# Weight sums of the projection pairs tied behind the C22 add, two mixed sums made in place, and one product's weight split on VectorE

## The chip, the cores and the metric

The kernel runs on one core of one Trainium2 chip. A core has five engines that this text speaks of: PE (TensorE, the matmuls), DVE (VectorE), ACT (ScalarE), POOL (GpSimd) and SP, which here only issues DMA transfers. Each engine works through its own instructions in order and waits on semaphores for the others. The metric is the device time of one execution in microseconds (us).

## The reference

Four layers over 1024 tokens of width 1024, all in fp32: an attention layer, a pooling layer, a mixer of two branches (neighbourhood attention and a gated recurrence, with 16 meta tokens put ahead of the sequence), and an MLP. The change concerns the pooling layer and three large projections of the rest:

```python
def pool_layer(h, w_in, w_mix, scale, w_out):
    u, z = jnp.split(h @ w_in, [POOL_WIDTH], axis=-1)
    p = multiscale_pool(u)          # per group: window sums of 2, 4, 8, 16 tokens / count - u
    m = jnp.einsum('bsgc,gcd->bsgd', p, w_mix).reshape(B, S, POOL_WIDTH) * scale
    return (m * jax.nn.silu(z)) @ w_out
...
    h = h + mix @ w_o[l]
    m = rms_norm(h, norm_mlp[l])
    h = h + jnp.square(jax.nn.relu(m @ w_up[l])) @ w_down[l]
```

## The kernel before

An fp32 operand X is held as two parts: hi, an ACT cast to a reduced fp32 form ("whi" for weights, "xh" for activations), and lo = X - hi ("wlo", "xl"), made by DVE or POOL. `mm3` makes a product from three matmuls, hi·hi, hi·lo and lo·hi. In the profile L108 is hi·hi, L110 and L111 are the two mixed ones. `split_evac` makes both parts; `split_b` (L249) does so for two halves of a weight block, its low part on POOL unless another engine is named.

Large products are done by seven block products in place of eight (Winograd's form of Strassen): with A cut into four blocks, S1 = A21 + A22, S2 = S1 - A11, S3 = A21 - A11, S4 = A12 - S2, the same kind of sums for the weights, and sums of the products for the result's blocks C11, C12, C21, C22.

**Input projections** (`project_pairs`, used for the pool layer's w_in with 8 pairs and for w_up with 16). A pair is 2 × 128 output columns. Its two products with A11 and A12 (`first_two`) come early for the first pairs (NF = 5 in the pool layer, 4 in the up projection), otherwise just ahead of the pair. Then, per pair, PE does S2, S1, S3, S4 and A22, twelve matmuls each. `weight_sums` (L361) makes the pair's four weight sums on DVE, from the raw weights that SP has loaded; `split_group` (L272) makes their parts, whi on ACT (L275), wlo on POOL (L276). Behind S3 DVE adds the bank to C22 (`res.add(p, "22", ...)`, L226 in the pool layer, L1853 in the up projection). The A22 product goes into the same bank, so PE waits for that add. The order in which DVE gets sums and adds is set by the code's order, a scheduler's priorities, and `tc.issue_after(x)`, which ties what is issued in it behind instruction x. For the first NF pairs x was the sums of the previous pair:

```python
                with tc.issue_after(ready.pop(p)):
                    done = weight_sums(r1, r2, tt)
                if p + 1 < NF:
                    ready[p + 1] = done
```

**The pool layer.** Even pairs give u, odd pairs silu(z); ACT copies banks (L898), the class `Pooled` cuts the window sums into small steps on DVE that it puts between the pair's instructions (`steps`), ending in a split ("cut", L950). After two pairs `mix` (L957) multiplies with w_mix, scales on DVE (L966), and makes the blocks of the next product's operand for a quarter q: A11, A12, A22 and S1 to S4, which it stores to memory (d_m). For the last quarter all of these went to memory too, and the output projection loaded S2, S1 and A22 whole into three tiles "ub" (`load_m`, 1 MB each).

**The output projections** (pool layer from L1080, w_o from L1797): seven products of 24 matmuls for the first and 24 for the second weight half, as three loops `times`; `split_a` makes the activations' parts, `less` the weight differences on DVE, `add_p` adds the banks to x. The third product takes S2 and w11 - w12. `made[0]` is the last low part that `split_a` made. In the pool layer the meta tokens' norm (an ACT square at L1107, and Newton steps of a reciprocal root on DVE, L124 to L132) stands between.

Of the kernel before, what the change touches and what calls it, by code (L numbers as in the profile page):

```python
# [19 lines left out]
P = 128  # L20
# [10 lines left out]
def fused_kernel(tc, a, out, stop=None, dbg=None):  # L31
# [295 lines left out]
    def project_pairs(w, col, npr, xx, sh, gcol, rows, a11, a12, stage, raw_tile, opened, res, w0, scaled, NF):  # L327
# [89 lines left out]
        for j in range(4):  # L417
            if j < 3:
                banks[j + 1] = [turned(rows[4:], j + 1 + k) for k in (0, 4)]
            if 0 < j < NF:  # L420
                open_[j] = first_two(j, wf[j])
            rest = sums(j)
            if j < 3:
                rest()
            if j == 0:
                split_first(2)
                split_first(3)
                if NF > 4:
# [399 lines left out]
    with ExitStack() as ph:  # L828
# [34 lines left out]
        class Pooled:  # L863
# [29 lines left out]

            def copy(self, p, key, ps):
                if key != "11":
                    self.steps(1)
                c_ = ea[:, p - 2, :] if p in EARLY and key == "11" else self.dst(p, key)
                nc.scalar.copy(out=c_, in_=ps)  # L898
                return c_
# [57 lines left out]
        def mix(g, q):  # L957
# [4 lines left out]
            for j, h in ((0, 0), (1, 0), (0, 1), (1, 1)):  # L962
# [13 lines left out]
            for n, c_, x_, y_, op in (("S3", m[0, 0], m[0, 1], m[0, 0], ALU.subtract),  # L976
                                      ("S1", m[0, 1], m[0, 1], m[1, 1], ALU.add), ("S2", s2, m[1, 1], m[0, 0], ALU.add),
                                      ("S4", m[1, 0], m[1, 0], s2, ALU.subtract)):
                vec(c_, x_, y_, op)
                nc.sync.dma_start(out=d_m[n][:, q, :], in_=c_)  # L980

# [30 lines left out]
        def load_x(h, ch):  # L1012
            for t in range(4 * h, 4 * h + 4):
                nc.sync.dma_start(out=X.at(t, ch), in_=d_x1[t][:, ch * 512:ch * 512 + 512])

        load_x(0, 0)
# [5 lines left out]
        ring = {}  # L1022

        def load_m(n):
            ring[n] = mp.tile([P, 4, 512], F32, name="ub", bufs=3)
            nc.sync.dma_start(out=ring[n], in_=d_m[n])

        load_m("S2")
        load_m("S1")
        load_x(0, 1)  # L1030
        load_m("A22")
        load_x(1, 1)
# [11 lines left out]
        def add_p(banks, h, ch, done=False, rows=range(4)):  # L1044

            for i in rows:
                t = 4 * h + i
                dst = X.at(t, ch)
                vec(dst, dst, banks[i], ALU.add)
                if done:  # L1050
# [50 lines left out]
        C = banks4()  # L1101
        times(C, *ops, True)
        ops = split_a("xl0", in_two(ring["S4"])), split_b(w22)
        with tc.issue_after(made[0].ins):
            mj = ea[:, 1:, :].rearrange("p a b -> p (a b)")
            sm_ = small.tile([P, 1], F32, name="ss")
            nc.scalar.activation(out=mj[:NM], in_=mt[:NM], func=AF.Square, accum_out=sm_[:NM])  # L1107
# [6 lines left out]
        for i in range(2):  # L1114
            split_evac(*t4[i], w21[i])
        add_p(C, 0, 1, True)
# [608 lines left out]
    with ExitStack() as ph:  # L1725
# [356 lines left out]
```

## Time and profile before

| what | value |
|---|---|
| median of the runs | 2394.87 us (2392.39 to 2399.99, 3 runs) |
| profiled execution | 2395.45 us |
| its span | 2393.6 us, 32247 instructions |
| mean granted TensorE clock | 0.984 |
| PE busy | 2290.5 us (96%) |
| DVE, ACT, POOL busy | 1509.4, 1021.5, 802.7 us |
| pool layer's input projection, from about | 470 to 680 us |
| its output projection | 680 to 780 us |
| w_o projection | 1640 to 1720 us |
| up projection, from about | 1765 us |

In the timelines a row is: start, duration, engine, line, operation, out<-in (partitions × elements, type), count, and in brackets the engine's idle time ahead of it and what ended it. A busy PE matmul of 512 columns lasts 0.39 us in the profile, but they overlap: one starts every 0.227 us when nothing is late.

### The profile page before, as it was taken

To read this page: it belongs to the slowest core of one execution; us is meant where nothing else is said; L and a number is where in the kernel's file an instruction comes from. 1 tells how busy PE (TensorE), PEld (TensorE's weight loads), DVE (VectorE), ACT (ScalarE), POOL (GpSimd) and SP (SyncE) were. 2 spreads that over 40 slices of the span, in tenths; PEclk is the share of its full clock that TensorE was granted. 3 is DMA by queue.
4 is the path that set the end of the run, shared out by engine and by line. 5 is a ranking of instruction groups with operands and counts; after the bars stand their busy time and mean duration, and the time that the engine had idled before them with its cause. 6 is when DMAs were issued, how large, how long until landed. Compare 5 with 4: busy or idle time off the path is not lost. (4 is left out here: it accounts for less than half of the span.)

```text
span 2393.6 us, 32247 instructions
## 1 busy us (share of the span) xinstructions
PE 2290.5 (96%) x11910; PEld 1904.0 (80%) x11910; DVE 1509.4 (63%) x2732; ACT 1021.5 (43%) x1921; POOL 802.7 (34%) x527
## 2 busy tenths in 40 slices
PE   7999999989988999999999999999889999999997
PEld 6877878767767888888988888887767888878886
DVE  5566676797678355554165746758784444686775
ACT  5344452643345354553232322423565555533334
POOL 2112133333433244331222112125414444454445
PEclk9999999989989999999999999999999999999999
DMA  5111113423372322211111111467135444764331
GB/s 159 36 28 36 28 32 106 145 67 119 101 252 79 93 58 54 67 50 54 45 45 53 49 53 49 135 197 266 64 121 198 149 147 167 257 227 167 106 123 71
DMA packets 249230, 254.41 MB, mean 106 GB/s; under 512 B 61096, under 2 KB 183038, under 8 KB 244848
## 3 DMA queue, kind: packets, MB, share of 16 engines
q1 hardware_dynamic: 240256, 234.69, 30.1%
q10 hardware_dynamic: 8224, 16.00, 1.7%
q0 software_dynamic: 592, 1.65, 0.4%
q8 instruction: 94, 1.54, 0.3%
q14 instruction: 64, 0.52, 0.1%
HBM read 182.05 MB, written 70.25 MB: 105 GB/s over the span
## 5 line engine op out<-in xcount | busy, mean ns | idle before, releaser
L108 PE MATMUL mm<-xh,whi 128*128 128x512 f32 (+2 forms) x1616 | 624.4, 387 | 18.2 <-DVE u L226 5.4
L110 PE MATMUL mm<-xl,whi 128*128 128x512 f32 (+2 forms) x1616 | 617.6, 382 | 0.0
L111 PE MATMUL mm<-xh,wlo 128*128 128x512 f32 (+2 forms) x1616 | 614.5, 380 | 1.9 <-POOL wlo L80 1.9
L80 POOL TENSOR_TENSOR wlo<-wraw,whi 128x1024 fp32r<-128x1024 f32 (+1 forms) x99 | 235.8, 2385 | 739.9 <-ACT whi L79 676.0
L108 PEld LDWEIGHTS mm<-xh,whi 128*128 128x128 f32 x1616 | 307.3, 190 | 77.0 <-DVE u L226 6.3
L111 PEld LDWEIGHTS mm<-xh,wlo 128*128 128x128 f32 x1616 | 306.9, 190 | 60.8 <-POOL wlo L80 2.7
L110 PEld LDWEIGHTS mm<-xl,whi 128*128 128x128 f32 x1616 | 307.4, 190 | 51.2
L111 PE MATMUL mm<-whi,xl 128*128 128x512 f32 (+1 forms) x752 | 273.3, 363 | 0.0
L79 ACT CAST whi<-wraw 128x1024 fp32r<-128x1024 f32 (+1 forms) x99 | 101.1, 1023 | 264.0 <-PE mm L110 146.0
L110 PE MATMUL mm<-wlo,xh 128*128 128x512 f32 (+1 forms) x560 | 196.9, 352 | 2.8 <-POOL wlo L80 1.4
L108 PE MATMUL mm<-whi,xh 128*128 128x512 f32 (+1 forms) x560 | 196.8, 352 | 2.5 <-DVE x L526 1.0
L108 PE MATMUL mm<-whi,xl 128*128 128x512 f32 x416 | 165.0, 398 | 13.5 <-ACT whi L118 8.2
L110 PE MATMUL mm<-wlo,xl 128*128 128x512 f32 x416 | 164.5, 396 | 10.7 <-POOL wlo L119 10.7
L276 POOL TENSOR_TENSOR wlo<-raw,whi 128x1024 fp32r<-128x1024 f32 (+1 forms) x59 | 121.5, 2059 | 137.8 <-ACT whi L275 137.7
L111 PEld LDWEIGHTS mm<-whi,xl 128*128 128x128 f32 x752 | 143.0, 190 | 22.1
L119 POOL TENSOR_TENSOR wlo<-wraw,whi 128x1024 fp32r<-128x1024 f32 x34 | 95.3, 2807 | 103.4 <-ACT whi L118 98.0
L110 PEld LDWEIGHTS mm<-wlo,xh 128*128 128x128 f32 x560 | 105.9, 189 | 17.8 <-POOL wlo L80 2.0
L108 PEld LDWEIGHTS mm<-whi,xh 128*128 128x128 f32 x560 | 105.9, 189 | 17.2 <-DVE x L526 1.4
L276 POOL TENSOR_TENSOR wlo<-wraw,whi 128x1024 fp32r<-128x1024 f32 (+1 forms) x28 | 70.9, 2534 | 136.5 <-ACT whi L275 109.0
L108 PEld LDWEIGHTS mm<-whi,xl 128*128 128x128 f32 x416 | 79.6, 192 | 32.3 <-ACT whi L118 7.7
L110 PEld LDWEIGHTS mm<-wlo,xl 128*128 128x128 f32 x416 | 79.6, 191 | 29.4 <-POOL wlo L119 13.1
L226 DVE TENSOR_TENSOR st<-st 128x512 f32<-128x512 f32 x64 | 63.2, 1008 | 56.7 <-ACT st L1928 55.6
(434 smaller groups left out, 4590.0 us busy)
## 6 DMA issues: line engine op xcount, KB each, us to landing
wraw<-in_w_in_dram SPq DMA_DIRECT2D x48, 512.0 KB, 3.7
d_S<-st SPq DMA_DIRECT2D x64, 256.0 KB, 4.5
raw<-in_w_up_dram SPq DMA_DIRECT2D x30, 512.0 KB, 5.4
d_A<-st ACTq DMA_DIRECT2D x48, 256.0 KB, 2.0
fa<-d_S SPq DMA_DIRECT2D x10, 1024.0 KB, 4.7
fa<-d_A SPq DMA_DIRECT2D x9, 1024.0 KB, 6.0
wraw<-in_attn_w_in_dram SPq DMA_DIRECT2D x32, 256.0 KB, 2.9
xh<-in_w_down_dram SPq DMA_DIRECT2D x16, 512.0 KB, 5.5
```

The source lines that it names most:

```text
L79: nc.scalar.copy(out=hv[:, i:i + n], in_=view[:, i:i + n])
L80: nc.gpsimd.tensor_tensor(out=lv[:, i:i + n], in0=view[:, i:i + n], in1=f(hv[:, i:i + n]), op=ALU.subtract)
L108: nc.tensor.matmul(ps, lhsT=lh[0], rhs=rh[0], start=first and i == 0, stop=False, skip_group_check=chain)
L110: nc.tensor.matmul(ps, lhsT=lh[0], rhs=rh[1], start=False, stop=False, skip_group_check=chain)
L111: nc.tensor.matmul(ps, lhsT=lh[1], rhs=rh[0], start=False, stop=last and i == n - 1, skip_group_check=chain)
L119: return (lo_eng or nc.vector).tensor_tensor(out=lo, in0=src, in1=f(hi), op=ALU.subtract)
L226: return nc.vector.tensor_tensor(out=out_, in0=x_, in1=y_, op=op)
L276: nc.gpsimd.tensor_tensor(out=lv, in0=view, in1=f(hv), op=ALU.subtract)
```

## The change

1. The weight sums of every pair (from the second on) are tied behind the C22 add of the pair before, in both input projections.
2. Pool layer: a bank is copied ahead of the pooled steps, not behind the first of them.
3. Pool layer, last quarter: S2 and S1 are written by DVE into the "ub" tiles themselves, and A22's quarter is copied there from its tile; the first three quarters are loaded ahead of the last mix.
4. The third product's low weights are made by DVE in place of POOL, in both output projections.
5. In the pool's output projection some DVE and ACT work is put or tied behind the banks' adds (`added`) or the last split (`made`): the splits of S3 and A22, the meta tokens' norm, two weight differences, the split of t4.

```diff
@@ project_pairs
-                ready = {1: weight_sums(*r0)}
+                weight_sums(*r0)
+                ready = {}
...
                 with tc.issue_after(ready.pop(p)):
-                    done = weight_sums(r1, r2, tt)
-                if p + 1 < NF:
-                    ready[p + 1] = done
+                    weight_sums(r1, r2, tt)
...
             res.add(p, "22", c22, b_)
-            if p + 1 >= NF:
-                ready[p + 1] = added[0].ins
+            ready[p + 1] = added[0].ins
@@ Pooled.copy
+                c_ = ea[:, p - 2, :] if p in EARLY and key == "11" else self.dst(p, key)
+                nc.scalar.copy(out=c_, in_=ps)
                 if key != "11":
                     self.steps(1)
-                c_ = ea[:, p - 2, :] if p in EARLY and key == "11" else self.dst(p, key)
-                nc.scalar.copy(out=c_, in_=ps)
@@ mix
-                            nc.sync.dma_start(out=d_m[n][:, q, :], in_=m[j, h])
-            s2 = s_tile()[:, :512]
+                            nc.sync.dma_start(out=d_m[n][:, q, :] if q < 3 else ring[n][:, 3, :], in_=m[j, h])
+            s2, s1 = [ring[n][:, 3, :] for n in ("S2", "S1")] if q == 3 else (s_tile()[:, :512], m[0, 1])
...
+                if q < 3 or n in ("S3", "S4"):
+                    nc.sync.dma_start(out=d_m[n][:, q, :], in_=c_)
@@ pool layer, output projection
+        for n in ("S2", "S1", "A22"):
+            load_m(n, 3)
         mix(GO[3], 3)
...
-        ops = o6, split_b(w11)
+        ops = o6, split_b(w11, nc.vector)
         o5 = split_a("xh0", in_two(ring["S1"]))
         load_m("S3")
-        less(w21, w21, w11)
-        less(w11, w22, w11)
+        with tc.issue_after(made[0].ins):
+            less(w21, w21, w11)
+            less(w11, w22, w11)
...
-        o4 = split_a("xh1", in_two(ring["A22"]))
...
-        with tc.issue_after(made[0].ins):
+        add_p(C, 1, 1)
+        times(C, *ops, False, True)
+        with tc.issue_after(added[0].ins):
+            o7 = split_a("xl1", in_two(ring["S3"]))
+            o4 = split_a("xh1", in_two(ring["A22"]))
             mj = ea[:, 1:, :].rearrange("p a b -> p (a b)")
...
-        add_p(C, 1, 1)
-        times(C, *ops, False, True)
-        ops = split_a("xl1", in_two(ring["S3"])), split_b(w12)
+        ops = o7, split_b(w12)
...
-            split_evac(*t4[i], w21[i])
+        with tc.issue_after(made[0].ins):
+            for i in range(2):
+                split_evac(*t4[i], w21[i])
@@ w_o, output projection
-        ops = o6, split_b(w11)
+        ops = o6, split_b(w11, nc.vector)
```

The lines of the changed kernel are one to two lower than before's between L434 and about L1100, and one higher behind.

DVE at pair 0 of the pool's input projection, before: the sums of pair 1 (raw_5247, wraw_5333, raw_5245) and of pair 2 (raw_5286, wraw_5451, raw_5318), and pair 0's C22 add, u_5266 with bank mm_4949.

```order
L226 TENSOR_TENSOR raw_5247<-raw_5247 128x512
L119 TENSOR_TENSOR s4l_4939<-sum_5014,s4h_4938 128x512
L226 TENSOR_TENSOR wraw_5333<-raw_5245,raw_5247 128x512
L226 TENSOR_TENSOR wraw_5333<-raw_5247,wraw_5333 128x512
L226 TENSOR_TENSOR raw_5245<-raw_5245,wraw_5333 128x512
L226 TENSOR_TENSOR raw_5286<-raw_5286 128x512
L226 TENSOR_TENSOR wraw_5451<-raw_5318,raw_5286 128x512
L226 TENSOR_TENSOR wraw_5451<-raw_5286,wraw_5451 128x512
L226 TENSOR_TENSOR u_5266<-u_5266,mm_4949 128x512
L226 TENSOR_TENSOR raw_5318<-raw_5318,wraw_5451 128x512
```

The same place now:

```order
L119 TENSOR_TENSOR s4l_4939<-sum_5014,s4h_4938 128x512
L226 TENSOR_TENSOR u_5266<-u_5266,mm_4949 128x512
L226 TENSOR_TENSOR raw_5247<-raw_5247 128x512
L226 TENSOR_TENSOR wraw_5333<-raw_5245,raw_5247 128x512
L226 TENSOR_TENSOR wraw_5333<-raw_5247,wraw_5333 128x512
L226 TENSOR_TENSOR raw_5245<-raw_5245,wraw_5333 128x512
L226 TENSOR_TENSOR u_5266<-u_5266,mm_5249 128x512
```

The add has moved ahead of all sums, and the sums of pair 2 have left this place.

DVE ahead of the third product of the pool's output projection, before: xl1 is the low part of S2 (loaded into ub_6433), wraw_6333 and wraw_6334 the two halves of w11, xh0_6588 the low part of S1, raw_63xx with mm the adds of the first product's banks.

```order
L226 TENSOR_TENSOR raw_6372<-raw_6372,mm_6456 128x512
L226 TENSOR_TENSOR raw_6369<-raw_6369,mm_6457 128x512
L119 TENSOR_TENSOR xl1_6519<-ub_6433,xl1_6519 128x1024 x2
L241 TENSOR_TENSOR wraw_6333<-wraw_6333,w12_6332 128x1024
L241 TENSOR_TENSOR wraw_6334<-wraw_6334,w12_6332 128x1024
L119 TENSOR_TENSOR xh0_6588<-ub_6435,xh0_6588 128x1024 x2
L241 TENSOR_TENSOR w21_6330<-w21_6330,wraw_6333 128x1024
```

Now (ub_6377 is S2, ub_6379 S1; z_6236 and z_6195 are tiles of the last mix):

```order
L226 TENSOR_TENSOR z_6195<-z_6195 128x512
L226 TENSOR_TENSOR ub_6379<-z_6195,z_6236 128x512
L226 TENSOR_TENSOR ub_6377<-z_6236,z_6195 128x512
L241 TENSOR_TENSOR w12_6332<-w12_6332,w22_6331 128x1024
L226 TENSOR_TENSOR z_6236<-z_6236,ub_6377 128x512
L241 TENSOR_TENSOR w12_6332<-w12_6332,w22_6331 128x1024
L119 TENSOR_TENSOR xl1_6516<-ub_6377,xl1_6516 128x1024 x2
L226 TENSOR_TENSOR raw_6369<-raw_6369,mm_6450 128x512
L226 TENSOR_TENSOR raw_6370<-raw_6370,mm_6451 128x512
L226 TENSOR_TENSOR raw_6371<-raw_6371,mm_6452 128x512
L226 TENSOR_TENSOR raw_6372<-raw_6372,mm_6453 128x512
```

S2's split has moved ahead of the first product's adds, right behind the sums that write it; the weight differences, half a split of S1 and the two low weight parts (wlo_6578, wlo_6582) follow there.

ACT at the same place, before:

```order
L118 CAST xh0_6337<-z_6195 128x512
L118 CAST whi_6509<-w21_6330 128x1024
L118 CAST xl0_6338<-z_6240 128x512
L118 CAST whi_6513<-w21_6330 128x1024
L1107 ACTIVATE ea_4192,ss_6745<-sum_6432 16x1024
L118 CAST xl1_6519<-ub_6433 128x1024 x2
```

and now:

```order
L118 CAST xh0_6337<-z_6195 128x512
L118 CAST whi_6506<-w21_6330 128x1024
L1109 ACTIVATE ea_4192,ss_6799<-sum_6435 16x1024
L118 CAST xl0_6338<-z_6236 128x512
L118 CAST whi_6510<-w21_6330 128x1024
L118 CAST xl1_6516<-ub_6377 128x1024 x2
```

The square of the meta tokens (L1107, now L1109) has moved ahead of the cast of xl from the last mixed tile.

More of the change, by code (lines that the diff above doesn't have):

```diff
@@ L973, in mix @@
                         if v == (j, h):
-                            nc.sync.dma_start(out=d_m[n][:, q, :], in_=m[j, h])
-            s2 = s_tile()[:, :512]
+                            nc.sync.dma_start(out=d_m[n][:, q, :] if q < 3 else ring[n][:, 3, :], in_=m[j, h])
+            s2, s1 = [ring[n][:, 3, :] for n in ("S2", "S1")] if q == 3 else (s_tile()[:, :512], m[0, 1])
             for n, c_, x_, y_, op in (("S3", m[0, 0], m[0, 1], m[0, 0], ALU.subtract),
-                                      ("S1", m[0, 1], m[0, 1], m[1, 1], ALU.add), ("S2", s2, m[1, 1], m[0, 0], ALU.add),
+                                      ("S2", s2, m[1, 1], m[0, 0], ALU.add), ("S1", s1, m[0, 1], m[1, 1], ALU.add),
                                       ("S4", m[1, 0], m[1, 0], s2, ALU.subtract)):
                 vec(c_, x_, y_, op)
-                nc.sync.dma_start(out=d_m[n][:, q, :], in_=c_)
+                if q < 3 or n in ("S3", "S4"):
+                    nc.sync.dma_start(out=d_m[n][:, q, :], in_=c_)
         wv = w_pout.rearrange("(q j p) c -> p q j c", j=2, p=P)
@@ L1014, in load_x, with load_m @@
                 nc.sync.dma_start(out=X.at(t, ch), in_=d_x1[t][:, ch * 512:ch * 512 + 512])
+        ring = {}
+        def load_m(n, nq=4):
+            ring[n] = mp.tile([P, 4, 512], F32, name="ub", bufs=3)
+            nc.sync.dma_start(out=ring[n][:, :nq, :], in_=d_m[n][:, :nq, :])
         load_x(0, 0)
+        for n in ("S2", "S1", "A22"):
+            load_m(n, 3)
         mix(GO[3], 3)
@@ L1021, in fused_kernel @@
         fg, mt = [s_tile()[:, :D] for _ in range(2)]
[L1022 to L1029, printed above, removed]
         load_x(0, 1)
-        load_m("A22")
         load_x(1, 1)
@@ L1048, in add_p @@
                 dst = X.at(t, ch)
-                vec(dst, dst, banks[i], ALU.add)
+                added[:] = [vec(dst, dst, banks[i], ALU.add)]
                 if done:
@@ L1109, in fused_kernel @@
             nc.vector.tensor_scalar_mul(mt[:NM], mt[:NM], r[:NM])
-        add_p(C, 1, 1)
-        times(C, *ops, False, True)
-        ops = split_a("xl1", in_two(ring["S3"])), split_b(w12)
+        ops = o7, split_b(w12)
         t4 = list(zip(*[in_two(mp.tile([P, 4, 512], F32R, name=n, bufs=b)) for n, b in (("ub", 3), ("w22", 1))]))
-        for i in range(2):
-            split_evac(*t4[i], w21[i])
+        with tc.issue_after(made[0].ins):
+            for i in range(2):
+                split_evac(*t4[i], w21[i])
         add_p(C, 0, 1, True)
```

## The prediction

> **What bounds the kernel now.** I read the page first, then the table of stretches, then the list of who waits for whom, and last the timeline of single engines around each wait. The first row of the page names the engine, and the table of stretches (microseconds of the stretch, then busy time of each engine, granted TensorE clock, DMA share, GB/s) shows where it is not full.
>
> ```profile
> PE 2290.5 (96%) x11910; PEld 1904.0 (80%) x11910; DVE 1509.4 (63%) x2732; ACT 1021.5 (43%) x1921; POOL 802.7 (34%) x527
> ```
>
> ```profile
> 470.00:680.00 210.00, 189.64 (x776) 151.60 (x775) 161.05 (x185) 83.43 (x122) 82.58 (x41) 0.94 0.37 114
> 680.00:780.00 100.00, 85.45 (x374) 68.60 (x373) 82.63 (x106) 50.84 (x95) 32.67 (x13) 0.93 0.43 147
> 780.00:1640.00 860.00, 847.56 (x5030) 728.62 (x5029) 474.73 (x986) 320.13 (x697) 230.08 (x189) 1.00 0.25 78
> 1640.00:1720.00 80.00, 68.13 (x280) 54.39 (x279) 63.72 (x59) 30.63 (x41) 52.08 (x20) 0.94 0.39 146
> 1765.00:1900.00 135.00, 127.53 (x544) 103.26 (x543) 74.65 (x95) 73.67 (x111) 56.98 (x27) 0.97 0.47 158
> ```
>
> PE is busy 96% of the span, and the long stretch from 780 to 1640 loses 12 us of 860 at clock 1.00. The four other stretches lose 20, 15, 12 and 7 us of idle time in 525, at a lower clock. They are the pool layer's input projection (470 to 680), its output projection (680 to 780), the w_o projection (1640 to 1720) and the up projection (from 1765), where the change acts. What PE waited for (total, times, longest):
>
> ```profile
> PE mm L110 <- POOL wlo L119: 11.7, 6, 6.9
> ...
> PE mm L108 <- ACT z L898: 5.8, 2, 3.9
> ...
> PE mm L108 <- DVE st L1853: 3.6, 3, 2.6
> ```
>
> A stall costs more than its length. Start times in the PE timeline, before, in and behind the stall at 511:
>
> ```profile
> 508.81 0.39 PE L111 MATMUL mm<-s4h,wlo 128*128 128x512 f32 x1
> ...
> 510.85 0.39 PE L111 MATMUL mm<-s4h,wlo 128*128 128x512 f32 x1
> 516.19 0.79 PE L108 MATMUL mm<-xh,whi 128*128 128x512 f32 x1 [4.95 <-DVE u L226]
> ...
> 522.22 0.39 PE L111 MATMUL mm<-s2h,wlo 128*128 128x512 f32 x1
> ```
>
> The nine steps from 508.81 to 510.85 are 0.227 us each. The fourteen from 516.19 to 522.22 take 6.03 us instead of 3.18: 2.85 us lost behind a gap of 5.34.
>
> **The weight sums of the pairs.** The four sums of pair p+1 used to follow those of pair p; now they wait for the C22 add of pair p. In pair 0 DVE did this:
>
> ```profile
> 509.92 2.86 DVE L226 TENSOR_TENSOR wraw<-raw 128x512 f32<-128x512 f32 x1
> 512.82 2.71 DVE L226 TENSOR_TENSOR wraw<-raw,wraw 128x512 f32<-128x512 f32 x1
> 515.46 0.67 DVE L226 TENSOR_TENSOR u<-u,mm 128x512 f32<-128x512 f32 x1
> ```
>
> Two sums of later pairs, stretched to four times their usual 0.68, stood ahead of the add that PE needed. With the add first, 5.1 us of the gap and the 2.85 us of slow matmuls go: 8 us. But the sums now start later, and pair 1's S2 product needs them through the add, the sums, the ACT cast and POOL's low part. Pair 7, whose sums were tied this way already, prices that chain:
>
> ```profile
> 638.03 0.69 DVE L226 TENSOR_TENSOR u<-u,mm 128x512 f32<-128x512 f32 x1 [2.75 <-PE mm L111]
> ```
>
> ```profile
> 642.01 3.50 POOL L276 TENSOR_TENSOR wlo<-wraw,whi 128x1024 fp32r<-128x1024 f32 x1 [3.43 <-ACT whi L275]
> ```
>
> From 638.03 to 645.5 are 7.5 us. Pair 7 hides them under its two opening products; the early pairs (pool 1 to 4, up 1 to 3) have their openings behind them, so the cover is S4, A22 and two matmuls of S2, 26 of 0.227 or 5.9 us. Odd pairs get a stall of 1.6 us; even pool pairs have a mix in between, 24 matmuls, that covers it. The mixes pay otherwise. POOL's low part now falls beside the pooled chain's two-input DVE work, which last time cost this, a 1.2 us split stretched to 3.1 and a PE wait behind it:
>
> ```profile
> 534.76 3.10 DVE L119 TENSOR_TENSOR u<-u,sum 128x1024 fp32r<-128x1024 f32 x1 [0.22 <-ACT sum L118]
> ```
>
> ```profile
> 537.91 0.49 PE L110 MATMUL mm<-u,whi 128*128 128x512 f32 x1 [1.87 <-DVE u L119]
> ...
> 539.18 0.63 PE L110 MATMUL mm<-u,whi 128*128 128x512 f32 x1
> ```
>
> On POOL the clearing of the next u tile, which waits for that split, now stands ahead of the mix weights' low part. I charge each of the first two mixes 2 us, one such wait (0 to 4), the odd pairs 1 and 3 together 3.2, and 1.6 us, a little over half of 2.85, for a slow pace behind one of these: 8.8 against 8 saved in pair 0. Pool pairs: 1 us lost (6 won if no new stall shows, 5 lost if both mixes pay 4).
>
> In the up projection PE waits for the same kind of add (st, L1853: 3.6 us in three waits). The longest, with the weight sum that stood ahead of its add:
>
> ```profile
> 1807.17 0.69 DVE L226 TENSOR_TENSOR wraw<-raw 128x512 f32<-128x512 f32 x1 [1.18 <-DMA raw<-in_w_up_dram]
> ```
>
> ```profile
> 1809.84 0.50 PE L108 MATMUL mm<-xh,whi 128*128 128x512 f32 x1 [2.60 <-DVE st L1853]
> ```
>
> The adds move ahead of the sums, so this wait of 2.6 us and the rest, 1.0 at most, go. But the long one mostly changes its place: its sums wait for a load that lands at 1807.1, and from there the chain (7.5 us less the add's 0.7) ends at 1813.9 at the worst, 2.4 sooner at the best with POOL and ACT free; without the stall S2's third matmul, 14 of 0.227 behind an A22 that starts at 1807.2, would be due at 1810.3. Gain 0.5 us (2 lost to 2 won).
>
> **S2 and S1 in place, and the third product's split.** The third product of the pool's output projection waited behind this chain (ACT, DVE, POOL, PE):
>
> ```profile
> 677.56 0.62 ACT L118 CAST xl<-z 128x512 fp32r<-128x512 f32 x1 [2.31 <-DVE z L966]
> ...
> 690.43 1.06 ACT L1107 ACTIVATE ea<-sum 16x1024 f32<-16x1024 f32 x1 [9.28 <-DMA sum<-in_meta_tokens_dram]
> ...
> 697.11 1.99 ACT L118 CAST xl<-ub 128x1024 fp32r<-128x1024 f32 x2 [5.53 <-DMA ub<-d_mS]
> ```
>
> ```profile
> 686.49 2.47 DVE L226 TENSOR_TENSOR raw<-raw,mm 128x512 f32<-128x512 f32 x4
> ...
> 698.19 2.36 DVE L119 TENSOR_TENSOR xl<-ub,xl 128x1024 fp32r<-128x1024 f32 x2 [5.21 <-ACT xl L118]
> ```
>
> ```profile
> 684.19 0.53 POOL L1037 DMA_DIRECT2D sum<-in_meta_tokens_dram  x1
> ```
>
> ```profile
> 673.48 0.39 PE L111 MATMUL mm<-sum,wlo 128*128 128x512 f32 x1
> ...
> 695.94 0.39 PE L111 MATMUL mm<-whi,xl 128*128 128x512 f32 x1
> ...
> 706.24 0.80 PE L110 MATMUL mm<-wlo,xl 128*128 128x512 f32 x1 [0.82 <-POOL wlo L119]
> ```
>
> The round trip of S2 through memory, ended at 697.1, goes: DVE writes the last quarter into the ring. What is late next is ACT: the meta tokens' square (L1107, now L1109) stands ahead of the cast of xl from z, and waits for a transfer that lands 6.2 us after POOL issues it (684.19 to 690.4). POOL issues it when the last mix's tiles are read, at 673.7, so it lands at 679.9; square 1.1, cast 0.6: DVE's low part of xl, due right behind the cast of 677.56, starts at 681.6. Five 128x512 instructions of 0.7 (that split and the four quarter sums) and two weight differences of 1.2 follow, with one stretch of 2.2 beside POOL's low part (as at 509.92); then the S2 split 2.36, four adds 2.47, two weight differences (128x1024 in two halves, so 2.36 again), a half split 1.2 and the first low weights 1.2: 699.3. That is 7 us ahead of 706.24. PE still stalls 3.4 us from 695.94, and its slow clock stays.
>
> The fifth product waited for C's adds, which stood behind two splits and the meta norm's Newton steps on DVE:
>
> ```profile
> 733.26 0.67 DVE L226 TENSOR_TENSOR z<-z,mm 128x512 f32<-128x512 f32 x1
> ```
>
> ```profile
> 728.67 0.39 PE L111 MATMUL mm<-whi,xh 128*128 128x512 f32 x1
> 734.07 0.76 PE L108 MATMUL mm<-whi,xl 128*128 128x512 f32 x1 [5.02 <-DVE w L128]
> ...
> 737.17 0.39 PE L110 MATMUL mm<-wlo,xl 128*128 128x512 f32 x1
> ```
>
> Now the adds come first: 5.2 us of the gap go, and 1.5 more, since the seven steps from 734.07 to 737.17 took 3.1 us instead of 1.6. Together 13.7 on PE, but the work passed over has to be done before the layer's norms, and DVE is busy 82.6 of the stretch's 100 us. I let 11 through (7 if only the third product's part reaches the norms, 14 if DVE hides all).
>
> In the w_o projection only the split's engine changes:
>
> ```profile
> 1674.62 9.59 POOL L119 TENSOR_TENSOR wlo<-wraw,whi 128x1024 fp32r<-128x1024 f32 x2 [5.47 <-issue]
> ```
>
> ```profile
> 1675.06 2.34 DVE L119 TENSOR_TENSOR xh<-a,xh 128x1024 fp32r<-128x1024 f32 x2
> ```
>
> ```profile
> 1674.55 0.48 PE L108 MATMUL mm<-whi,xl 128*128 128x512 f32 x1
> 1681.93 0.79 PE L110 MATMUL mm<-wlo,xl 128*128 128x512 f32 x1 [6.90 <-POOL wlo L119]
> ```
>
> DVE now makes half of the split at 1675.06, then the first low weights: 1675.06 + 1.2 + 1.2 = 1677.4 against 1681.9, so 4.5 us (3 if DVE is stretched by another 1.5, 6 if 1.5 of slow matmuls goes too). The second half comes two such steps later, and 24 matmuls of the first half, 5.4 us, cover it. PE's gap becomes 2.9 us; the wait of 1.9 at 537.91 was followed by matmuls of 0.63 at 539.18, so I keep the slow clock. The Trainium skill, "TensorE: Matmul & The Clock Gate", Part 1, lets the clock drop only after an idle window of about 3.4 us, which this row contradicts. By that rule the gap of 2.9 us here and the 3.4 left ahead of the third product would cost nothing behind them.
>
> Pool's bank copies put ahead of the pooled steps gain nothing: on ACT the copies still stand behind the split's cast at pairs 5 and 7, so the 5.8 us on L898 stay.
>
> Sum against the profiled execution of 2395.45 (span 2393.6 and 1.85 around it; 0.6 above the median 2394.87): 11 + 4.5 + 0.5 - 1 = 15. That gives 2380.4, or 2379.9 on the median's scale; I say 2380.
>
> **Rivals.** *All pair stalls go*: the new chains stay under cover, pool pairs win 6, up 2, the projection 13: 25 us, 2370. For it speaks that pair 7's 7.5 us contains a stretched POOL instruction; against it, pooled work that now lies exactly there. *Short gaps at full clock*: gaps up to 3.4 us are followed by matmuls of 0.39 at once, against the row at 539.18; two such gaps give 1.5 each, the charge of 1.6 in pool pairs falls away too: 4.6 us more, 2375. This is what the rule of the Trainium skill named above ("TensorE: Matmul & The Clock Gate", Part 1) comes to here. *ACT holds up the third product*: the square's transfer lands 4 us later than worked out, the third product starts at 703.3, and DVE's backlog of those 4 us makes the fifth and the norms as late again, 5 in all: 15 - 9 = 6, or 2389. It is decided at 681.6: each microsecond later there is one later on PE. *Slower*: the tied sums' chain, in the five pairs without cover (pool 1 and 3, up 1 to 3) and the two mixes. Once it exceeds 7.8 us, PE's wait exceeds 1.9 and the slow pace follows. With POOL's low part at 4.8, as in the two of 1674.62, instead of 3.5, the chain is 8.8: 2.9 and 2 of slow matmuls in each of five, 24.5, and the mixes 4 each, 32.5; less 8 and 2.6 of stalls removed, 22 lost against 15.5 won in the projections: 6.5 slower, 2401. Against it: only the pool's DVE is that crowded, and 638.03 shows 7.5 there. *The change doesn't do what it says*: the copies above are such a part, with no price.
>
> **Chances.** Forecast 0.58 (8 to 23 us won: 2372 to 2387), all stalls go 0.12, full clock 0.06, third product held up 0.12, slower 0.07, none of these 0.05. The range 2366 to 2392 takes in the first four. A measurement can tell 0.3%, about 7 us, from no change. Faster: 0.58 + 0.12 + 0.06 and a part of the held-up case, 0.78; same 0.15; slower 0.07.
>
> **What would show it.** Right: no PE gap at pair 0's A22 product, short waits on POOL's L276 at S2 of odd pairs; the third product starting near 699 with its low weights from DVE; no gap ahead of the fifth; a gap of 3 us instead of 7.4 in w_o. Wrong: PE gaps above 2.3 us at three or more S2 products; the mixes waiting above 4 us; the cast of xl from z after 684.

## The result and the profile after

The changed kernel takes 2381.62 us (2379.26 to 2383.87), the kernel before 2394.93 in the same job: a ratio of 0.9942, 95% interval 0.9923 to 0.9961, 13.3 us. A second job gave 2383.16 against 2392.71, 0.9959 (0.9945 to 0.9972). The profiled execution has a span of 2380.7 us against 2393.6. The first row of its page, then three of the stretches of the prediction (busy time of PE, PEld, DVE, ACT, POOL, granted clock, DMA share, GB/s):

```profile
PE 2284.9 (96%) x11910; PEld 1898.1 (80%) x11910; DVE 1505.3 (63%) x2736; ACT 1022.0 (43%) x1921; POOL 782.3 (33%) x523
```

```profile
470.00:680.00 210.00, 186.99 (x780) 148.32 (x779) 159.64 (x187) 85.05 (x125) 81.72 (x43) 0.97 0.38 120
680.00:780.00 100.00, 90.66 (x414) 73.59 (x414) 84.78 (x142) 54.73 (x104) 23.50 (x10) 0.97 0.37 133
1640.00:1720.00 80.00, 72.96 (x319) 58.52 (x318) 66.84 (x70) 37.89 (x57) 37.21 (x16) 0.98 0.32 118
```

PE starts 40 more matmuls than before in the 100 us from 680, 39 more in the 80 from 1640, but only 4 more in the 210 from 470: the gain is in the two output projections. What PE waits for now:

```profile
PE mm L108 <- ACT z L894: 8.3, 3, 3.9
...
PE mm L111 <- POOL wlo L276: 5.9, 7, 1.3
PE mm L1074 <- DVE sum L1111: 5.5, 1, 5.5
PE mm L110 <- POOL wlo L119: 5.4, 4, 2.0
...
PE mm L108 <- ACT whi L79: 4.0, 2, 3.4
```

The wait on wlo L119 fell from 11.7 to 5.4 us, its longest from 6.9 to 2.0. Seven short waits on the pairs' low weights (L276) stand where before had two; new are one of 5.5 us for the meta tokens' norm (L1111), a third one for a bank copy (L894, before L898) and one of 3.4 on a mix's weights (L79).

To place the gain I put the PE instructions of each profile in order of their starts; all have 11910. The table gives, for the instruction that before reaches at the time on the left, how much earlier the other kernel starts it (us). The columns are the changed kernel and the runs told below; "2nd" is the changed kernel in the second job.

```
before at            after  2nd    e1    e2    e3    e4    e5    e6    e7    e8    e9   e10   e11
470 pool pairs begin  -0.1   0.3   0.2  -0.1  -0.8  -0.7  -0.1   0.2   0.3   1.6   0.8   0.3   0.0
520 behind pair 0      7.8   8.1   8.1   7.8   6.6   6.3   7.9   8.2   8.0   9.4   8.6   8.2   7.9
565 ahead of mix 2     5.7   5.6   6.0   5.7   4.6   4.2   5.8   3.5   5.4   6.9   7.7   7.2   7.7
585 behind mix 2       0.5   0.9   0.9   0.5  -0.8  -0.9   0.6   1.1   0.8   2.3   4.3   3.8   4.1
680 projection out     0.7   1.2   1.1   0.7  -0.6  -0.6   0.8   1.3   1.1   2.5   4.5   4.1   3.8
707 third product     10.4  10.9   0.5  10.5   7.9   3.6  10.0  11.0  10.1   4.2  14.2  13.8  13.5
735 fifth product     16.2  17.1   0.5  16.7  13.7   8.8  15.8  17.3  15.9  10.9  20.3  19.7  19.4
765 norms              8.5   9.6  -0.1  13.0   6.6   1.9   6.8   9.4   7.3   5.0  12.9  14.4  15.7
1640 w_o begins        8.3   9.1   0.0  13.1   6.4   0.6   6.4   9.3   6.1   3.8  10.9  13.9  15.3
1685 its third product 14.5  14.6   0.2  18.1  10.6   5.9   5.9  14.0  11.2   9.6  14.8  18.9  20.5
1720 w_o ends         11.9  12.1   0.1  17.4   9.5   3.3   4.9  13.8   8.6   7.1  14.5  18.1  18.0
2393 end              12.5  13.3   0.5  19.0  10.2   4.3   5.2  13.8   9.3   8.5  15.6  19.8  19.3
```

Differences of one or two microseconds between columns mean little: the leads at 470, where no edit lies ahead, go from -0.8 to 1.6, and after, 2nd, e6 and e7 reach the norms with 8.5, 9.6, 9.4 and 7.3, though nothing but the pairs differs between them.

**The pairs.** Pair 0's long gap is gone, and the short one that was foretold stands at pair 1's S2 (PE, DVE and POOL of the changed kernel):

```profile
510.15 0.39 PE L111 MATMUL mm<-s4h,wlo 128*128 128x512 f32 x1
510.38 0.39 PE L108 MATMUL mm<-xh,whi 128*128 128x512 f32 x1
...
513.32 0.39 PE L110 MATMUL mm<-s2l,whi 128*128 128x512 f32 x1
514.39 0.50 PE L111 MATMUL mm<-s2h,wlo 128*128 128x512 f32 x1 [0.67 <-POOL wlo L276]
```

```profile
507.93 0.69 DVE L226 TENSOR_TENSOR u<-u,mm 128x512 f32<-128x512 f32 x1 [2.02 <-PE mm L111]
...
511.96 3.47 DVE L226 TENSOR_TENSOR sum<-u 128x1039 f32<-128x1039 f32 x1
515.47 5.56 DVE L226 TENSOR_TENSOR sum<-sum 128x1037 f32<-128x1037 f32 x2
```

```profile
511.94 2.39 POOL L276 TENSOR_TENSOR wlo<-wraw,whi 128x1024 fp32r<-128x1024 f32 x1 [9.23 <-ACT whi L275]
514.29 5.65 POOL L276 TENSOR_TENSOR wlo<-raw,whi 128x1024 fp32r<-128x1024 f32 x2
```

The last two rows of DVE are the next loss. Three pooled sums, 1.23 us each where POOL is idle (as at 520.95), take 9.0 while POOL makes the pair's low parts. The pooled chain ends late, and ACT, which takes its work in order, keeps a bank copy behind the chain's cast; PE's S4 product waits for the bank (ACT, then PE):

```profile
523.56 1.04 ACT L118 CAST sum<-u 128x1024 fp32r<-128x1024 f32 x1 [5.99 <-DVE u L226]
524.51 0.58 ACT L894 COPY z<-mm 128x512 f32<-128x512 f32 x1
...
525.14 0.67 PE L108 MATMUL mm<-s4h,whi 128*128 128x512 f32 x1 [2.75 <-ACT z L894]
```

At pair 3 and the second mix behind it the same collision costs 5.2 us (5.7 to 0.5 in the table). DVE's sums are held up again; first pair 3's own C22 add, then the mix's operand, come late (DVE, then PE):

```profile
554.77 6.83 DVE L226 TENSOR_TENSOR sum<-sum 128x1037 f32<-128x1037 f32 x3
...
573.59 1.22 DVE L119 TENSOR_TENSOR u<-u,sum 128x1024 fp32r<-128x1024 f32 x1
```

```profile
567.03 0.50 PE L108 MATMUL mm<-xh,whi 128*128 128x512 f32 x1 [2.60 <-DVE z L226]
...
569.66 0.39 PE L111 MATMUL mm<-xh,wlo 128*128 128x512 f32 x1
573.45 0.79 PE L108 MATMUL mm<-sum,whi 128*128 128x512 f32 x1 [3.40 <-ACT whi L79]
574.86 0.79 PE L110 MATMUL mm<-u,whi 128*128 128x512 f32 x1 [0.62 <-DVE u L119]
```

**The pool's output projection.** The third product no longer waits; PE runs through 695 at 0.227 us a step, and the slow matmuls that before had behind its wait, up to 709.8, are gone too. The meta transfer lands earlier than before, and the low weights are ready at 695.5 (POOL, ACT, DVE):

```profile
672.75 0.55 POOL L1035 DMA_DIRECT2D sum<-in_meta_tokens_dram  x1 [13.39 <-PE mm L111]
```

```profile
677.08 1.06 ACT L1109 ACTIVATE ea<-sum 16x1024 f32<-16x1024 f32 x1 [2.54 <-DMA sum<-in_meta_tokens_dram]
...
678.13 0.60 ACT L118 CAST xl<-z 128x512 fp32r<-128x512 f32 x1
```

```profile
694.34 2.35 DVE L119 TENSOR_TENSOR wlo<-wraw,whi 128x1024 fp32r<-128x1024 f32 x2
```

The fifth product's gap has shrunk but isn't gone; a second wait, on POOL's low weights, has come up behind it:

```profile
718.32 0.47 PE L108 MATMUL mm<-whi,xl 128*128 128x512 f32 x1 [0.87 <-DVE z L226]
...
721.85 0.50 PE L110 MATMUL mm<-wlo,xl 128*128 128x512 f32 x1 [1.68 <-POOL wlo L119]
```

Half of the 16 us is then lost ahead of the norms. The meta tokens' norm has been tied behind C's adds and comes last on DVE; PE, which works in order, waits with the transposes of those tokens (DVE, POOL, PE):

```profile
733.72 2.07 DVE L128 SCALAR_TENSOR_TENSOR w<-r,hx 16x1 f32<-16x1 f32 x1
735.82 2.27 DVE L132 SCALAR_TENSOR_TENSOR r<-w,r 16x1 f32<-16x1 f32 x1
...
738.62 0.73 DVE L1111 TENSOR_SCALAR sum<-sum,r 16x1024 f32<-16x1024 f32 x1
```

```profile
733.43 2.35 POOL L119 TENSOR_TENSOR wlo<-w,whi 128x1024 fp32r<-128x1024 f32 x1 [8.30 <-ACT whi L118]
735.74 2.34 POOL L80 TENSOR_TENSOR wlo<-wraw,whi 128x1024 fp32r<-128x1024 f32 x1
```

```profile
739.41 1.03 PE L1074 MATMUL mm<-ident,sum 16*128 16x16 f32 x8 [5.50 <-DVE sum L1111]
```

**w_o.** The wait for the third product's low weights fell from 6.9 to 0.9 us in this execution, and matmuls of 0.39 follow at once. It now ends with DVE's low part:

```profile
1668.90 0.50 PE L110 MATMUL mm<-wlo,xl 128*128 128x512 f32 x1 [0.89 <-DVE wlo L119]
```

### The profile page after: what moved, and what is told of

It reads as the page before. It is cut to its first block, busy times and chain, and to the rows that moved or that the text cites. A ratio compares the mean times of both kernels' runs of the same rounds, so it can differ in the third digit from the quotient of the medians.

```text
span 2380.7 us, 32233 instructions
## 1 busy us (share of the span) xinstructions
PE 2284.9 (96%) x11910; PEld 1898.1 (80%) x11910; DVE 1505.3 (63%) x2736; ACT 1022.0 (43%) x1921; POOL 782.3 (33%) x523
## 5 line engine op out<-in xcount | busy, mean ns | idle before, releaser
L80 POOL TENSOR_TENSOR wlo<-wraw,whi 128x1024 fp32r<-128x1024 f32 (+1 forms) x99 | 232.4, 2350 | 734.0 <-ACT whi L79 631.9
L79 ACT CAST whi<-wraw 128x1024 fp32r<-128x1024 f32 (+1 forms) x99 | 101.2, 1023 | 267.1 <-PE mm L110 145.5
L276 POOL TENSOR_TENSOR wlo<-raw,whi 128x1024 fp32r<-128x1024 f32 (+1 forms) x59 | 125.5, 2131 | 110.2 <-ACT whi L275 110.2
L276 POOL TENSOR_TENSOR wlo<-wraw,whi 128x1024 fp32r<-128x1024 f32 (+1 forms) x28 | 68.2, 2440 | 154.1 <-ACT whi L275 126.6
L119 POOL TENSOR_TENSOR wlo<-wraw,whi 128x1024 fp32r<-128x1024 f32 x30 | 78.3, 2613 | 104.5 <-ACT whi L118 104.4
```

The source lines that it names most:

```text
L79: nc.scalar.copy(out=hv[:, i:i + n], in_=view[:, i:i + n])
L80: nc.gpsimd.tensor_tensor(out=lv[:, i:i + n], in0=view[:, i:i + n], in1=f(hv[:, i:i + n]), op=ALU.subtract)
L119: return (lo_eng or nc.vector).tensor_tensor(out=lo, in0=src, in1=f(hi), op=ALU.subtract)
L276: nc.gpsimd.tensor_tensor(out=lv, in0=view, in1=f(hv), op=ALU.subtract)
```

## The experiments

All but the first start from the changed kernel; times are medians, ratios are against the kernel before in the same job.

**One part alone: the ties.**

```diff
  (in the kernel before)
-                ready = {1: weight_sums(*r0)}
+                weight_sums(*r0)
+                ready = {}
...
-            if p + 1 >= NF:
-                ready[p + 1] = added[0].ins
+            ready[p + 1] = added[0].ins
```

> The kernel before, with the weight sums of every pair tied behind the C22 add and nothing else. Theory (the tie gains about 8 us at pair 0 and the pool layer's two mixes and odd pairs give nearly all of it back, since DVE's pooled chain and POOL's low parts now fall together): PE 7 to 8 us ahead of before behind pair 0, 5 to 6 ahead behind the first mix, under 1.5 ahead when the pool pairs end; the up projection adds 0.5 to 1; total 1 to 2 us faster than before, about 2393. Rival (the tie is what the changed kernel's gain comes from, and its loss at the second mix comes from the other edits, such as the bank copy ahead of the pooled steps): 5 to 8 us ahead when the pool pairs end, total 2387 to 2389.

2394.95 us against 2393.82, 1.0001 (0.9992 to 1.0010): no difference, where 1 to 2 us were foretold. Column e1 shows why, and the theory holds there: 8 us are won in pair 0, 2 go ahead of the second mix and 5 in it, and the rest of the program is as before. The 13 us come from the output projections.

**The third product's parts, each undone alone.**

```diff
  (e4: pool's output projection)
-        ops = o6, split_b(w11, nc.vector)
+        ops = o6, split_b(w11)
```

> The changed kernel, with the third product's low weights of the pool layer's output projection back on POOL. Theory (most of the third product's gain is S2 made in place; DVE's split is worth what POOL's stretched instructions cost above DVE's 1.2 us each): the third product starts 1 to 4 us later than in the changed kernel, and since PE then waits for the meta tokens anyway, the total is within 1.5 us of it. Rival (the split on DVE is the gain): the third product starts 6 us or more later and the total is 3 us or more slower.

```diff
  (e8: last quarter of S2, S1 and A22 through memory, loaded whole)
-            s2, s1 = [ring[n][:, 3, :] for n in ("S2", "S1")] if q == 3 else (s_tile()[:, :512], m[0, 1])
+            s2, s1 = s_tile()[:, :512], m[0, 1]
...
+        load_m("S2")
+        load_m("S1")
         load_x(0, 1)
+        load_m("A22")
```

> The changed kernel, with the last quarter of S2, S1 and A22 stored to memory and the three tiles loaded whole, as before; everything else as changed. Theory (the round trip ends at about 697 and was most of the third product's lateness): the third product starts 6 to 8 us later than in the changed kernel, near 703; the meta tokens' wait shrinks by part of it, and the total is 2 to 5 us slower, 2384 to 2387. Rival (the meta tokens' wait is the only bound at the end of that projection): the total is within 1 us.

e4 takes 2387.29 us, 0.9972 (0.9963 to 0.9981); e8 takes 2386.95, 0.9975 (0.9965 to 0.9986). Each is 4 to 6 us over the changed kernel's two medians. For e4 the theory missed and the rival's price came true; for e8 the theory held. The first rows are POOL and PE of e4, the others ACT and PE of e8:

```profile
694.58 9.04 POOL L119 TENSOR_TENSOR wlo<-wraw,whi 128x1024 fp32r<-128x1024 f32 x2 [9.78 <-ACT whi L118]
```

```profile
701.34 0.79 PE L110 MATMUL mm<-wlo,xl 128*128 128x512 f32 x1 [4.17 <-POOL wlo L119]
```

```profile
694.02 1.99 ACT L118 CAST xl<-ub 128x1024 fp32r<-128x1024 f32 x2 [5.91 <-DMA ub<-d_mS]
```

```profile
699.72 2.08 PE L108 MATMUL mm<-whi,xl 128*128 128x512 f32 x4 [5.88 <-ACT whi L118]
```

So the third product waits for the later of two chains, the activations' and the weights'. From 680 to 707 the changed kernel wins 9.7 us, e4, with the in-place sums alone, 4.2, and e8, with the split on DVE alone, 1.7: together they win more than the two apart. No run undoes the order of C's adds, the fifth product's part, alone: its worth is read off the profiles. POOL needs 4.5 us for a low part of 2.4 here, beside a busy DVE.

**w_o's split back on POOL.**

```diff
  (w_o)
-        ops = o6, split_b(w11, nc.vector)
+        ops = o6, split_b(w11)
```

> The changed kernel, with the third product's low weights of the w_o projection back on POOL. Theory (the change won 4.5 us there and lost about 2.5 of what PE then held at the fifth product): 3 to 4 us slower than the changed kernel, 2385 to 2386, with a gap of 7 us on PE ahead of the third product and no gap at the fifth. Rival (the gain is taken back by the norms, which end when they did): within 1 us.

2385.64 us, 0.9968 (0.9957 to 0.9979), 2.5 to 4 us over the changed kernel. PE waits as before the change:

```profile
1676.07 0.79 PE L110 MATMUL mm<-wlo,xl 128*128 128x512 f32 x1 [6.90 <-POOL wlo L119]
```

**Where the meta tokens' norm stands.** In e2 it is tied ahead of C's adds, where before had it; in e3 PE's transposes of these tokens are moved into the loop behind.

```diff
  (e2)
+        with tc.issue_after(made[0].ins):
+            (square, reciprocal root and scaling of the meta tokens)
         add_p(C, 1, 1)
```

> The changed kernel, with the meta tokens' norm tied and placed as it was before (behind the split of S4, ahead of C's second adds); the splits of S3 and A22 stay behind the adds. Theory (the 5.5 us that PE waits for the meta tokens' transposes come from the meta norm's nine small DVE instructions standing behind two splits, t4's split and the adds): that wait falls under 1 us, the fifth product starts at most 1.5 us later than in the changed kernel, and the kernel is 4 to 6 us faster than the changed one, 2376 to 2378. Rival (the norms of the tokens themselves, not the meta rows, end the stretch, DVE being nearly full): the wait goes but the stall turns up at the transposes of the normed tokens; within 1.5 us of the changed kernel, 2380 to 2383.

```diff
  (e3)
         scaled = second_norms(0, 4)
-        meta_into_xt()
...
+            if n == 2:
+                meta_into_xt()
```

> The changed kernel, with the meta tokens' transposes on PE issued three rounds of the last products later (ahead of the first turned token blocks), and their norm on DVE left where the change put it. Theory (PE waits only because the transposes stand in its queue ahead of ready matmuls): the 5.5 us wait goes, 4 to 6 us faster than the changed kernel, 2376 to 2378. Rival (DVE is the bound there, so the wait returns at the token transposes): within 1.5 us of the changed kernel.

e2 takes 2378.05 us, 0.9938 (0.9926 to 0.9949). Its median is 3.6 and 5.1 us under the changed kernel's two, though its interval overlaps with theirs. In its profile the Newton steps run from 713.9 to 715.5, between two of POOL's low parts, the wait on L1111 is gone, and the lead at the norms is 13.0 instead of 8.5 to 9.6. e3 takes 2383.52, 0.9955 (0.9943 to 0.9967), no gain: PE then waits behind the same DVE work, for the layer's norms.

```profile
753.71 1.42 PE L282 MATMUL mm<-ident,raw 128*128 128x128 f32 x10 [3.35 <-DVE raw L308]
```

So it is DVE's order that costs, not PE's.

**The collision in the pairs: order or contention?** e6 ties only pair 1 and leaves the others in before's chain. e9 keeps all ties and makes two of the low parts of each of pairs 1 to 3 on DVE.

```diff
  (e6)
-            ready[p + 1] = added[0].ins
+            if not p or p + 1 >= NF:
+                ready[p + 1] = added[0].ins
```

> The changed kernel, with only pair 1's weight sums tied behind pair 0's C22 add; pairs 2 on follow the sums of the pair before, as they did before the change. Theory (the 8 us are won at pair 0 alone, and the 5 us lost at the second mix come from pair 4's sums and their POOL parts falling into the pooled chain of the pair before): PE 7 to 8 us ahead of before behind pair 0 and still 4 or more ahead when the pool pairs end; 3 to 5 us faster than the changed kernel, 2377 to 2379, less up to 1 us in the up projection. Rival (any order loses there, because DVE and POOL have the same work to do in the same stretch): ahead by under 1.5 us when the pool pairs end, total within 1.5 us of the changed kernel.

```diff
  (e9)
-            g = split_group(tt, KT)
+            low = nc.vector if NF == 5 and p in (1, 2, 3) else nc.gpsimd
+            g = split_group(tt, KT, low)
...
-            g = split_group(r2, KT)
+            g = split_group(r2, KT, low)
```

> The changed kernel, with the low weight parts of the pool layer's pairs 1 to 3 (S2 and S1 from tt, S3 and S4 from r2) made by DVE in place of POOL. Theory (what the pairs lose again at the two mixes is the stretching of DVE's two-input instructions beside POOL's low parts, 5 us of DVE time at the second pooled chain, more than the 1.2 us each that DVE would need for the parts themselves): no wait on POOL's low parts at S2 of pairs 1 and 3, PE 2 to 5 us further ahead than the changed kernel behind the second mix, total 2 to 5 us faster, 2377 to 2380. Rival (DVE has simply too much work there, whoever stands beside it): PE loses another 2 to 5 us at the mixes, since six instructions of 1.2 us come on top; total 2 us or more slower than the changed kernel.

e6 takes 2384.05 us, 0.9959 (0.9948 to 0.9971), and wins 0.8 us from 470 to 585, the changed kernel 0.6: another order of the sums only moves the loss, and e6's theory missed. e9 wins 3.5 there. Its DVE has more to do and is still done 3.3 us sooner (570.28 against 573.59, 0.9 of it the start of the stage), since it is held up less:

```profile
554.66 3.76 DVE L226 TENSOR_TENSOR sum<-sum 128x1037 f32<-128x1037 f32 x3
...
570.28 1.23 DVE L119 TENSOR_TENSOR u<-u,sum 128x1024 fp32r<-128x1024 f32 x1
```

The place and the mechanism are shown; the gain in time is not clear of noise. e9's median is 2381.58, 0.9949 (0.9937 to 0.9962), as in the changed kernel's first job and 1.6 us under its second, which was e9's own. In its profile the lead over the changed kernel is 3.8 at 680, 4.3 at the norms, 2.6 at w_o and 3.1 at the end. The medians show less, and one reason is that the profiled execution is e9's fastest of five (2379.59), the changed kernel's the second slowest of four (2382.49).

**The bank copies behind the pooled steps again.**

```diff
  (e7)
-                nc.scalar.copy(out=c_, in_=ps)
                 if key != "11":
                     self.steps(1)
+                nc.scalar.copy(out=c_, in_=ps)
```

> The changed kernel, with the bank copy back behind the first pooled step. Theory (ACT still has the split's cast ahead of the copies at pairs 5 and 7, so the edit is worth nothing): within 1 us of the changed kernel, and the waits on the copies the same. Rival (the edit takes part in the order of the second mix): the pool pairs end 1 to 5 us earlier or later.

2382.53 us, 0.9948 (0.9931 to 0.9965): between the changed kernel's two medians. PE waits for the copies 8.3 us in three waits, as with the copies ahead.

**The changed kernel again, and the two improvements together.**

> The changed kernel itself, unchanged, so that the next two are compared with it on the same chip: 2380 to 2383.

> The changed kernel, with both the meta tokens' norm placed early (as in e2_meta_early) and the low weight parts of pairs 1 to 3 on DVE (as in e9_low_on_dve). If both theories hold, the two gains add, since the places are 130 us apart on PE: 5 to 9 us faster than the changed kernel, 2373 to 2377. If only the meta norm counts, 3 to 5 us faster.

```diff
  (e11: e10, and every odd pair loads its mix weights early)
-                if p == 7:
-                    self.wm = w_rows(w_mix[GO[3]], 0, 2, 0, 256)
+                if p % 2:
+                    self.wm = w_rows(w_mix[GO[p // 2]], 0, 2, 0, 256)
```

> e10_both, with the mix weights of every group loaded at the end of the odd pair ahead of it (as the last group's already were), which puts their cast on ACT ahead of the casts that split the pooled sums. Theory (what is left of the waits at the first two mixes is this cast, 7.9 us in two waits, queued on ACT behind the pooled split, which itself comes late from DVE): the first matmul of both mixes no longer waits for that cast; it then waits for the pooled split instead, one cast of 1 us and one DVE split of 1.2 us, so only 1 to 3 us are won; PE 1 to 3 us further ahead than e10_both behind the second mix, total 2374 to 2377. Rival (the pooled sums on DVE end the wait whatever the order on ACT): within 1 us of e10_both at that point and in total.

e10 (e2 and e9) takes 2377.15 us, 0.9932 (0.9920 to 0.9945), 6.0 under the changed kernel in the same job; all five of its executions (2375.41 to 2378.48) lie below all five of that kernel (2381.71 to 2384.30). e11 takes 2375.99, 0.9930 (0.9915 to 0.9945), the lowest median of all, 6 to 7 us under the changed kernel; it can't be told from e10 or e2. The waits of PE from 480 to 680, of e10 and then of e11, show that the early weights only change the wait's name, as e11's rival said:

```profile
PE mm L108 <- ACT whi L79: 7.9, 2, 5.1
```

```profile
PE mm L108 <- ACT sum L118: 6.4, 2, 4.6
```

The cast of the weights (L79) stood behind the cast of the pooled sum (L118) on ACT; it is the pooled chain on DVE that is late.

## Why the prediction was right, and where not

The time came out 1.6 us from the forecast, in part by luck: by the rows of the table, the sum put the pairs 1.8 and the third product 2.7 us too low, and the loss ahead of the norms 5.0 too small. By the column "after", with the prediction's terms (another 0.2 goes between the norms and w_o):

| term | predicted, us | measured, us |
|---|---|---|
| pool pairs | -1 | +0.8 |
| third product | +7 | +9.7 |
| fifth product | +6.7 | +5.8 |
| lost ahead of the norms | -2.7 | -7.7 |
| w_o | +4.5 | +3.6 (2.5 to 4.6 in the other profiles with this split on DVE) |
| up projection | +0.5 | +0.6 |
| bank copies | 0 | 0 (e7) |

The rows at 707 and 735 stand inside the two products. The slow matmuls of before end at 709.8, so 1.2 us of what the table gives the fifth product belong to the third, and the new wait of 1.68 falls behind 735. Counted at before's 711 and 744, behind the slow pace of each, the third product won 10.9, the fifth 3.6 where 6.7 were foretold, and 6.7 were lost ahead of the norms. So "no gap ahead of the fifth" came true only in part: PE gets there sooner than DVE's adds and POOL's low weights. In e4 and e8, where it gets there later, the same stretch gives 6.6 and 6.7.

**Pairs.** The 8 us of pair 0 were right to 0.1. The chain from add to low part took 6.4 us (507.93 to 514.33), not 7.5: POOL's part took 2.39, where in pair 7 it was stretched to 3.50. So each odd pair pays 0.8 us in place of 1.6. "All pair stalls go" failed at the mixes and the "slower" rival with the chain: at the S2 products of pool pairs 1 and 3 and up pairs 1 to 3, the ones without cover, no wait is over 0.7 us, and no slow pace follows there. The charge of 2 us for each of the first two mixes had the right cause, POOL's low parts beside the pooled chain, but was unevenly spread: 2.1 from 520 to 565, mostly through a bank copy that the prediction had not seen, and 5.2 up to 585, through pair 3's add, not seen either, and the second mix, whose waits of 3.40 and 0.62 us reach the 4 that were named as a sign of error. e6 and e9 bear the cause out.

**Third product.** Mechanism as worked out; the term was mis-sized, mainly in one step. The meta transfer was charged 6.2 us from issue to landing; it took 4.3 (672.75 to 677.08). The cast of xl is at 678.13, not 681.0, DVE is held 0.65 us by it, and the low weights come at 695.5, not 699.3. A wait of 3.4 us and the slow pace behind it were foretold, neither is there. "ACT holds up the third product" was the wrong way round.

**Norms.** Here a step failed: "I let 11 through" priced what DVE had passed over at 2.7 us by a look at its load, without asking who waits for each piece of it. The piece that came last was the meta norm, and PE's own transposes stand behind it. A wait of 5.5 us, with matmuls at a slow pace behind it (granted clock 0.89 from 735 to 765), made it 7.7. e2 puts that norm earlier and loses 3.7 in the same place (16.7 to 13.0); counted from before's 744 it loses 2.7, what the prediction charged.

**w_o.** The split's price was right, the gap was not what made it up in this execution: PE came there later itself, and waited 0.9 us. In ten other profiles with this split on DVE the foretold gap is there, a wait of 2.42 or 2.43 us in place of 6.90. The slow pace that the prediction kept follows in five of them (e2, e3, e6, e9, e10) and not in the other five (2nd, e4, e7, e8, e11). In e2:

```profile
1661.56 0.49 PE L108 MATMUL mm<-whi,xl 128*128 128x512 f32 x1
1664.47 0.50 PE L110 MATMUL mm<-wlo,xl 128*128 128x512 f32 x1 [2.42 <-DVE wlo L119]
...
1665.27 0.62 PE L110 MATMUL mm<-wlo,xl 128*128 128x512 f32 x1
```

The eight steps from 1665.27 to 1668.67 take 3.4 us where 1.8 is the usual. The granted clock tells why. In these profiles it is 1 or 0.5, and it changes only at the edges of a grid of 3.41 us. The stretches around this gap (granted clock ahead of the DMA share):

```profile
1661.85:1665.26 3.41, 0.99 (x4) 0.67 (x4) 3.41 (x4) 1.04 (x1) 0.00 (x0) 1.00 0.00 0
1665.26:1668.67 3.41, 3.41 (x9) 2.64 (x8) 3.41 (x4) 1.04 (x1) 0.00 (x0) 0.50 0.00 0
```

The wait lies inside one grid step, PE is idle for 2.4 us of it, and the next step is granted at half clock. In the other five profiles an edge of the grid splits the wait, into at most 1.7 us in one step. So it is for the gap of 3.0 us that ends at 567.03 in the changed kernel: an edge at 566.27 leaves 1.8 us of idle time ahead of it and 0.8 behind, and the pace stays usual up to 569.66. From 470 to 2355 us of the 14 profiles, half clock followed each of the 105 grid steps at full clock in which PE was idle for 2 us or more, and none of the 7392 with 1.6 or less.

So "Short gaps at full clock" falls as a rule for gaps of this length, and so does "I keep the slow clock": what counts is the idle time within one step of the grid, which neither asked for. With it falls what the Trainium skill, "TensorE: Matmul & The Clock Gate", Part 1, would make of it: an idle window of about 3.4 us was not needed here. The 3.4 us are borne out as the length of the grid's steps.

Some 3 us (behind before's 1691) are given back at w_o's fifth product in six of the twelve profiles that follow the change (after, 2nd, e4, e7, e8, e11) and at most 0.5 in the others. The six are those in which no half clock follows the third product's gap. PE comes some 1.6 us sooner there and waits 1.7 for the first of DVE's adds of Xb (L1751; 1.73 in after). POOL's next low part falls beside the split that DVE makes between the first two adds: that split takes 3.2 us in each of the six, and 1.2 in e2, e3, e6, e9 and e10, so the second add is late as well. The traces show this; no edit was made to test it.

**Up projection.** The waits changed their place, as foretold. PE's waits from 1755 to 1900, before and then after:

```profile
PE mm L108 <- DVE st L1853: 3.3, 2, 2.6
```

```profile
PE mm L111 <- POOL wlo L276: 3.3, 4, 1.3
```

## What to carry to other kernels

When work is put off to let something urgent pass, write down for each piece who waits for it, the bottleneck engine's own next instructions among them, and put what nobody waits for last. A product waits for the later of its operands' chains: an edit to one of them shows its full worth only with the other one mended. And count DVE work whose two operands are both tiles, beside POOL, at about the sum of both, not the longer of the two; an add that takes one operand from a bank is not held up so.

## What the runs showed of the hardware

A DVE instruction that reads two tiles waits for a POOL low part already under way to end, whatever its own size. A Newton step on 16x1 elements, 0.2 us elsewhere, took 2.07 us: it ends at 735.79, and the POOL instruction beside it at 735.78. The next took 2.27 and ends at 738.09, POOL's at 738.08. The pooled sum of 511.96 ends 1.1 us behind POOL's end at 514.33, about its own length. POOL is held up in turn: 4.5 us for a low part of 2.4 in e4. An add that takes one operand from a bank (mm) is not held. In the changed kernel one add of two tiles took 1.35 us, and three adds of banks right behind it 0.62 each, all beside two low parts on POOL (DVE, then POOL):

```profile
704.08 1.35 DVE L226 TENSOR_TENSOR raw<-raw,sum 128x512 f32<-128x512 f32 x1
705.36 1.87 DVE L226 TENSOR_TENSOR raw<-raw,mm 128x512 f32<-128x512 f32 x3
```

```profile
702.47 5.24 POOL L119 TENSOR_TENSOR wlo<-wraw,whi 128x1024 fp32r<-128x1024 f32 x2 [19.55 <-ACT whi L118]
```

I had priced such a meeting as a stretch by some factor. The Trainium skill, "SBUF — State Buffer", section "SBUF: two separate sides", calls the port pair that DVE and GpSimd share an exclusive lock, held for the whole instruction, against a DVE instruction with two SBUF inputs. The Newton steps agree with it to 0.01 us.
